# A seventh-product scheme in a down projection: two more groups, and the sums of activations formed earlier

## The chip, the core and the metric

The kernel runs on one core of one Trainium2 chip. The number that counts is the device time of one execution in microseconds (us), the median over repeated runs, lower being better. A core has a matrix engine (PE, with its weight loads shown as PEld), a vector engine (DVE), a scalar engine (ACT), GpSimd (POOL) and SyncE (SP). They run beside each other and wait for one another through semaphores. In this kernel SP issues nearly all loads from HBM, in the order of its own queue, and POOL issues the stores of sums.

## What is computed

One layer of a hybrid transformer block for 256 positions of width 2048: an input projection, three kinds of attention, a gated merge, an output projection, then a feed-forward part. The change lies in the feed-forward part, in its last product and in what prepares it:

```python
h2 = rms_norm(x, g_ffn[l])
u = causal_depthwise_conv(h2 @ w_up[l], conv_w[l], conv_b[l])      # 2048 -> 2 x 5632
u_gate, u_val = jnp.split(u, 2, axis=-1)
x = x + (jax.nn.silu(u_gate) * u_val) @ w_down[l]                  # 5632 -> 2048
```

All of it is in float32. The kernel splits each float32 number into a high and a low float32r part and makes each product of three matmuls: high x high, low x high, high x low.

## The kernel before

**The up projection (L1219, L1221).** The loop runs over 11 blocks of four feature tiles (`f0`), twice each (`s` = 0 for the gate half, 1 for the value half), and over 8 pairs of k tiles: 176 passes, called ticks here. A tick loads 512 KB of weights (`raw_u`, issued by SP at L172, four buffers), ACT casts them to the high part (`hi_u`, L175), DVE subtracts to get the low part (`lo_u`, L176), both in rings of four buffers, and PE runs 16 matmuls. The order of the loads `raw_u` against other loads on SP is left to a scheduler.

**The convolution (`conv`, L1136 to L1163).** After each half of a block two generators are queued, one for each pair of feature tiles; they advance at most one step a tick. ACT and DVE apply taps and bias (`cr`, `u`, `z`, `y`). In the value half DVE multiplies by the gate (L1156) and the result is split into `aT`, which stays in SBUF (L1160, L1163).

**Sums of weights (`weight_sums`, L1177 to L1193).** The down projection treats some pairs of k tiles ("groups") by a scheme with seven products in the place of eight. It needs four sums of weight blocks. Two of them (T4 and T2), or all four, are made on DVE during the up projection: every seventh tick a new group loads its four 128x512 blocks on SP's queue into `r` (first the tile `r[1]` with two buffers, then `r[0]` with one), DVE adds, and POOL stores 512 KB to HBM as `T`. A group with all four (in the set `ALL_FOUR`) has one more add and a store of `r[0]` itself (L1191), so that the next group's loads into `r[0]` have to wait on SP's queue until this store has landed.

**The down projection (L1252 to L1471).** It runs in two halves of 1024 output columns. `PLANS` sets the order by hand: `e` is a group of eight products (`eight`: two loads of 512 KB, 24 matmuls of 128x512), `s` one of seven (`seven`: 21 matmuls, four steps p0 to p3 that prepare weights and u0 to u3 that use them). Steps are prepared two ahead (`AHEAD`). A group without its T1 and T3 in HBM makes them by two adds on DVE (L1371, L1372). The scheme also needs four sums of activations for each pair, its forms. They are made in this stage by `forms(p)`, on DVE and ACT: five adds and subtractions, two casts, two subtractions for the low part (L1273 to L1285). They serve both halves.

Of the kernel before, what the change touches and what calls it, by code (L numbers as in the profile page):

```python
# [37 lines left out]
PLANS = ("eeeee" + "se" * 5 + "sse" + "s" + "eee", "e" + "sse" * 4 + "ssse" + "sssee")  # L38
ALL_FOUR = {(0, 6), (0, 7)} | {(1, p) for p in range(14) if p not in (4, 6, 8, 11)}
# [10 lines left out]
NSEVEN = tuple(plan.count("s") for plan in PLANS)  # L50
# [3 lines left out]
def hybrid_block(  # L54
# [1075 lines left out]
    def conv(ps, f, s):  # L1130
# [20 lines left out]
        if s == 0:  # L1151
            nc.scalar.activation(y, y, AF.Silu)
            ys[f] = y
        else:
            g = ys.pop(f)
            nc.vector.tensor_tensor(g, g, y, ALU.mult)  # L1156
# [6 lines left out]
            nc.vector.tensor_tensor(a[:, :, S:], g, a[:, :, :S].bitcast(F32), ALU.subtract)  # L1163
            ended.append(f)

    ended = []
    made = {}
    asked = [(0, p) for p in range(NSEVEN[0])] + [(1, p) for p in range(NSEVEN[1])]

    def weight_sums(nb, p):  # L1170
# [11 lines left out]
        four = (nb, p) in ALL_FOUR  # L1182
# [24 lines left out]
    for f0 in range(0, FT, 4):  # L1207
        for s in range(2):
            pairs = [two_banks(f"u{f0 + i}_{s}") for i in (0, 2)]
            c0 = s * D_FF + f0 * P  # L1210
            for k in range(0, KT, 2):
# [11 lines left out]
                if asked and n_ticks[0] > 8 and n_ticks[0] % 7 == 2:  # L1223
                    adding.append([weight_sums(*asked.pop(0)), 0])
# [22 lines left out]
    FS3, FS1, FS2, FS4 = range(4)  # L1247
# [8 lines left out]
    def form_of(p, f):  # L1256
        if f == FS4:
            return pieces_of(p)[:, 0, :, 1]
        if p < 10:
            return sf[:, p, f]  # L1260
        return pieces_at(31 - p).rearrange("p k (f l q) -> p (k f) l q", f=2, l=2)[:, f]

    def forms(p):

        flat = aT[:, 2 * p : 2 * p + 3].rearrange("p k s -> p (k s)").bitcast(F32)
        v = flat[:, :1024].rearrange("p (k l t q) -> p k l t q", k=2, l=2, t=NT)
        d = sm.tile([P, 512], F32, tag="junk", bufs=2, name=f"fd_{p}").rearrange("p (f l q) -> p f l q", f=2, l=2)
        r = down_pool().tile([P, 512], F32, tag="fr", bufs=1, name=f"fr_{p}").rearrange("p (f q) -> p f q", f=4)
        g = rbc.rearrange("p (k q) -> p k q", k=2)
        two = flat[:, : 2 * 640].rearrange("p (a b) -> p a b", b=640)[:, :, :512]  # L1270
        two = two.rearrange("p a (l t q) -> p a l t q", l=2, t=NT)[:, :, :, 0]
        tt = nc.vector.tensor_tensor
        keep(tt(d, two, v[:, 0, :, 1].unsqueeze(1).to_broadcast([P, 2, 2, P]), ALU.subtract))  # L1273
        keep(tt(g, v[:, :, 0, 0], v[:, :, 1, 0], ALU.add))
        keep(tt(r[:, :2], d[:, :, 0], d[:, :, 1], ALU.add))
        keep(nc.vector.scalar_tensor_tensor(r[:, FS2], r[:, FS1], -1.0, g[:, 0], ALU.mult, ALU.subtract))
        keep(tt(r[:, FS4], r[:, FS2], g[:, 1], ALU.add))
        yield
        to = sf[:, p] if p < 10 else form_of(p, slice(0, 3))
        last = form_of(p, FS4)  # L1280
        keep(nc.scalar.copy(to[:, :, 0], r[:, :3]))
        keep(nc.scalar.copy(last[:, 0], r[:, FS4]))
        yield
        keep(tt(to[:, :, 1], r[:, :3], to[:, :, 0].bitcast(F32), ALU.subtract))
        keep(tt(last[:, 1], r[:, FS4], last[:, 0].bitcast(F32), ALU.subtract))  # L1285
# [64 lines left out]
    def seven(p, n0, X, Y, first, last):  # L1350
# [3 lines left out]
        four = (n0 // PIECE, p) in ALL_FOUR  # L1354
# [10 lines left out]
        def p2():  # L1365
            raw[2] = load(made[n0 // PIECE, p][0], f"t{name}")
            raw[3] = down_pool().tile([P, PIECE], F32, tag="t13", bufs=2, name=f"t13_{name}")
            if four:
                keep(nc.sync.dma_start(raw[3], made[n0 // PIECE, p][1]))
            else:  # L1370
                keep(nc.vector.tensor_tensor(raw[3][:, :512], raw[0][:, :512], raw[0][:, 512:], ALU.add))  # L1371
                keep(nc.vector.tensor_tensor(raw[3][:, 512:], raw[0][:, 512:], raw[1][:, 512:], ALU.add))  # L1372
            w["T4"], w["T2"] = parts(raw[2], f"t42_{name}")
# [7 lines left out]
        def u1():  # L1381
            three(X()[0][0], *a_of(k1, 0), w["10"])
# [64 lines left out]
    formed = 0  # L1447
# [5 lines left out]
    for nb, plan in enumerate(PLANS):  # L1453
        n0 = nb * PIECE
        ns, s = plan.count("s"), 0
# [3 lines left out]
        if nb == 0:  # L1459
            at(-1, lambda: start(0))  # L1460
        for i, c in enumerate(plan):
            if c == "s":
                seven(s, n0, X, Y, s == 0, s == ns - 1)
                s += 1
                if s == ns:
                    at(len(steps) - 1, lambda nb=nb: later(gather(nb, banks[nb][1])))
            else:
# [4 lines left out]
                if formed < ns and n_done >= 4 - 3 * nb:  # L1472
                    at(len(steps) - 2, lambda p=formed: later(forms(p)))
                    formed += 1
        assert s == ns and not straight and formed >= ns
# [49 lines left out]
```

## Time and profile before

| | |
|---|---|
| device time, median of 3 runs | 1472.15 us (1470.21 to 1473.51) |
| span of the profiled execution (first to last instruction) | 1469.9 us |
| mean granted clock of the matrix engine | 0.999 of full speed |
| busy share of the span: PE, PEld, DVE, ACT, POOL | 100%, 84%, 82%, 61%, 5% |
| up projection's ticks, first matmul to last | about 748 to 1241 us of the span |
| down projection's matmuls | 1241 to 1466 us of the span |
| groups by seven | 8 in the first half, 14 in the second |

The profile gives the span of the profiled execution alone; the runs' times also hold what lies around the span, about 2 us. The page's busy time of PE overlaps neighbouring matmuls, so it says that PE had always something in hand, not that it ran at its peak; the distance between starts is what a matmul costs.

### The profile page before, as it was taken

How to read it: one execution, taken by the hardware profiler on the slowest of the kernel's cores; microseconds unless marked ns; L12 is line 12 of the kernel's file. 1: busy time of each engine (PE TensorE's matmuls, PEld its weight loads, DVE VectorE, ACT ScalarE, POOL GpSimd, SP SyncE). 2: the span in 40 equal slices, each digit the busy share in tenths (PEclk: the TensorE clock that was granted, in tenths of full speed). 3: DMA queues.
4: the chain of work that ended last, by engine and by line, in shares of the span. 5: the costliest groups of instructions: out<-in, count | busy, mean ns of one | idle time of the engine just before them, and what ended most of it. 6: DMA issues, size and time to landing. Idle time of an engine off the chain costs nothing.

```text
span 1469.9 us, 20741 instructions
## 1 busy us (share of the span) xinstructions
PE 1462.8 (100%) x7327; PEld 1233.4 (84%) x7327; DVE 1205.1 (82%) x1617; ACT 895.3 (61%) x1287; POOL 68.8 (5%) x139
## 2 busy tenths in 40 slices
PE   9999999999999999999999999999999999999998
PEld 7888888888878888888888888888888888888887
DVE  5798767766997799888877888788887886998998
ACT  6755454454664466545657667567676777665774
POOL 1000001021000000000000000000000010000000
PEclk9999999999999999999999999999999999999999
DMA  8697898787766576866776888889888895778995
GB/s 295 202 341 260 265 313 270 226 294 267 256 221 204 204 271 247 287 222 237 273 239 218 302 272 276 294 277 310 295 265 273 280 305 190 249 256 286 334 315 191
DMA packets 163463, 388.81 MB, mean 265 GB/s; under 512 B 14016, under 2 KB 22512, under 8 KB 163360
## 3 DMA queue, kind: packets, MB, share of 16 engines
q1 hardware_dynamic: 150960, 345.34, 70.6%
q0 software_dynamic: 11648, 41.10, 7.3%
q8 instruction: 57, 0.93, 0.3%
q10 hardware_dynamic: 752, 1.06, 0.2%
q14 instruction: 46, 0.38, 0.1%
HBM read 349.70 MB, written 37.75 MB: 264 GB/s over the span
## 4 chain that ended last, share of the span: by engine, by line
PE 94%; DVE 3%; DMA 2%; issue 1%; ACT 0%; SPq 0%; DVEq 0%; ACTq 0%
PE u L1219 21%; PE u L1221 10%; PE d L1310 5%; PE d L1309 5%; PE d L1311 5%; PE g_x L769 4%; PE g_x L770 4%; PE g_x L771 4%; PE s L186 2%; PE s L188 2%; PE f L187 2%; PE f L188 2%; PE f L186 2%; PE s L187 2%; PE b L186 2%; PE b L188 2%
## 5 line engine op out<-in xcount | busy, mean ns | idle before, releaser
L1219 PE MATMUL u<-hT,hi_u 128*128 128x512 f32 x1408 | 442.6, 396 | 0.0
L1221 PEld LDWEIGHTS u<-hT,lo_u 128*128 128x128 f32 x1408 | 264.4, 188 | 63.5 <-DVE lo_u L176 1.1
L1221 PE MATMUL u<-hT,lo_u 128*128 128x256 f32 x1408 | 277.0, 278 | 0.7 <-DVE lo_u L176 0.7
L176 DVE TENSOR_TENSOR lo_u<-raw_u,hi_u 128x1024 fp32r<-128x1024 f32 x176 | 213.2, 1220 | 59.8 <-ACT hi_u L175 59.0
L175 ACT CAST hi_u<-raw_u 128x1024 fp32r<-128x1024 f32 x176 | 183.0, 1049 | 107.0 <-PE u L1219 54.6
L1219 PEld LDWEIGHTS u<-hT,hi_u 128*128 128x128 f32 x1408 | 214.5, 189 | 0.1
L764 ACT CAST hi_g<-raw_g 128x1024 fp32r<-128x1024 f32 (+1 forms) x96 | 91.1, 964 | 53.5 <-PE g_x L770 33.4
L765 DVE TENSOR_TENSOR lo_g<-raw_g,hi_g 128x1024 fp32r<-128x1024 f32 (+1 forms) x96 | 105.0, 1116 | 20.9 <-ACT hi_g L764 20.8
L769 PE MATMUL g_x<-hi_g,xT 128*128 128x512 f32 x251 | 98.8, 394 | 0.0
L770 PE MATMUL g_x<-hi_g,xT 128*128 128x512 f32 x251 | 97.7, 389 | 0.0
L771 PE MATMUL g_x<-lo_g,xT 128*128 128x512 f32 x251 | 96.3, 390 | 0.0
L1148 DVE TENSOR_TENSOR y<-y,z 128x512 f32<-128x512 f32 x88 | 60.7, 691 | 24.4 <-ACT z L1147 20.5
L1147 ACT ACTIVATE z<-u,taps 128x256 f32<-128x256 f32 x176 | 74.7, 496 | 0.0
L1309 PE MATMUL d<-hi_d,aT 128*128 128x512 f32 x176 | 68.5, 389 | 0.0
L1310 PE MATMUL d<-hi_d,aT 128*128 128x512 f32 x176 | 68.5, 389 | 0.0
L1311 PE MATMUL d<-lo_d,aT 128*128 128x512 f32 x176 | 68.1, 389 | 0.0
L175 ACT CAST hi_f<-raw_f 128x1024 fp32r<-128x1024 f32 (+1 forms) x40 | 38.6, 968 | 46.6 <-PE f L187 41.9
L186 PE MATMUL s<-hi_s,xT 128*128 128x512 f32 (+1 forms) x160 | 61.9, 387 | 0.0
L175 ACT CAST hi_b<-raw_b 128x1024 fp32r<-128x1024 f32 x32 | 33.6, 1052 | 45.2 <-PE b L187 23.5
L175 ACT CAST hi_s<-raw_s 128x1024 fp32r<-128x1024 f32 (+1 forms) x40 | 38.3, 959 | 36.8 <-PE s L187 29.3
L186 PE MATMUL f<-hi_f,xT 128*128 128x512 f32 (+1 forms) x160 | 60.4, 377 | 0.0
L188 PE MATMUL s<-lo_s,xT 128*128 128x512 f32 (+1 forms) x160 | 59.1, 369 | 0.0
(498 smaller groups left out, 3265.0 us busy)
## 6 DMA issues: line engine op xcount, KB each, us to landing
raw_u<-in_w_up_dram SPq DMA_DIRECT2D x176, 512.0 KB, 5.4
raw_g<-in_w_in_dram SPq DMA_DIRECT2D x86, 512.0 KB, 5.4
T<-r POOLq DMA_DIRECT2D x64, 512.0 KB, 6.1
r<-in_w_down_dram SPq DMA_DIRECT2D x88, 256.0 KB, 5.2
raw_d<-in_w_down_dram SPq DMA_DIRECT2D x44, 512.0 KB, 5.4
raw_f<-in_w_in_dram SPq DMA_DIRECT2D x32, 512.0 KB, 5.5
raw_s<-in_w_in_dram SPq DMA_DIRECT2D x32, 512.0 KB, 5.4
raw_s<-in_w_down_dram SPq DMA_DIRECT2D x32, 512.0 KB, 5.3
```

Source lines behind the costliest of these rows:

```text
L175: pin(nc.scalar.copy(hi[:, :m], raw[:, :m]))
L176: pin(nc.vector.tensor_tensor(lo[:, :m], raw[:, :m], hi[:, :m].bitcast(F32), ALU.subtract))
L186: nc.tensor.matmul(o, lhsT=xh, rhs=wh, start=first, stop=False)
L188: nc.tensor.matmul(o, lhsT=xh, rhs=wl, start=False, stop=last)
L769: nc.tensor.matmul(o, lhsT=a[0], rhs=w[0], start=first, stop=False)
L770: nc.tensor.matmul(o, lhsT=a[1], rhs=w[0], start=False, stop=False)
L771: nc.tensor.matmul(o, lhsT=a[0], rhs=w[1], start=False, stop=last)
L1219: nc.tensor.matmul(ps, lhsT=hi[:, j, c], rhs=hT[:, k + j, :], start=first, stop=False)
L1221: nc.tensor.matmul(ps[:, :S], lhsT=lo[:, j, c], rhs=hT[:, k + j, :S], start=False, stop=last)
L1309: nc.tensor.matmul(o, lhsT=ah, rhs=w[0], start=first, stop=False)
L1310: nc.tensor.matmul(o, lhsT=al, rhs=w[0], start=False, stop=False)
L1311: nc.tensor.matmul(o, lhsT=ah, rhs=w[1], start=False, stop=last)
```

## The change

Five things are done together.

1. The first half gets ten groups by seven (it had eight), the second keeps fourteen; two groups by eight go. The letter in the plan now tells the kind: `t` has two weight sums from HBM and makes the other two, `f` has all four from HBM. There are 15 of `t` and 9 of `f` (before: 10 and 12), all ten of the first half being `t`.
2. A new group of `weight_sums` starts every sixth tick, where it was every seventh.
3. The forms of the first 14 pairs are made in `conv`, from the product before its split, by three instructions on DVE (`unsplit_forms`), written over `y`, and stored by POOL to HBM, 256 KB a pair.
4. In the down projection `forms(i)` loads two pairs' forms with one load of 512 KB on SP's queue and splits them: two casts on ACT, two subtractions on DVE for the two pairs.
5. The two sums of a `t` group are written over its own weights (`raw[0]`) and have no tile of their own; extra load buffers go from two to four and are taken every second time.

```diff
-PLANS = ("eeeee" + "se" * 5 + "sse" + "s" + "eee", "e" + "sse" * 4 + "ssse" + "sssee")
-ALL_FOUR = {(0, 6), (0, 7)} | {(1, p) for p in range(14) if p not in (4, 6, 8, 11)}
+PLANS = ("eeee" + "tte" * 4 + "te" * 2 + "ee", "e" + "ftfe" * 4 + "ft" + "eee")
...
             ended.append(f)
+            if f // 2 < NFORM:
+                yield 1
+                unsplit_forms(f // 2, g, y)
+
+    def unsplit_forms(p, g, y):
+        v = g.rearrange("p k (t q) -> p (k t) q", t=NT)
+        r = y.rearrange("p k (t q) -> p (k t) q", t=NT)
+        tt = nc.vector.tensor_tensor
+        tt(r[:, :2], v[:, 0:4:3], v[:, 1:2].to_broadcast([P, 2, P]), ALU.subtract)
+        nc.vector.scalar_tensor_tensor(r[:, FS2], r[:, FS1], -1.0, v[:, 0], ALU.mult, ALU.subtract)
+        tt(r[:, FS4], r[:, FS2], v[:, 2], ALU.add)
+        if p % 2 == 0:
+            rforms[p // 2] = dram.tile([P, 2, 512], F32, name=f"rform{p}")
+        nc.gpsimd.dma_start(rforms[p // 2][:, p % 2], y.rearrange("p k s -> p (k s)"))
...
-                if asked and n_ticks[0] > 8 and n_ticks[0] % 7 == 2:
+                if asked and n_ticks[0] > 8 and n_ticks[0] % 6 == 2:
...
-        if turn[0] > 10 and turn[0] % 3 == 0:
-            return down_pool().tile([P, PIECE], F32, tag="more", bufs=2, name=name)
+        if turn[0] > 10 and turn[0] % 2 == 0:
+            return down_pool().tile([P, PIECE], F32, tag="more", bufs=4, name=name)
...
+    def forms(i):
+        p = 2 * i
+        n = min(2, NFORM - p)
+        raw = load(rforms[i][:, :n].rearrange("p a n -> p (a n)"), f"fr_{i}")
+        ...
+        yield 2
+        keep(nc.scalar.copy(to[:, :, :, 0], r[:, :, :3]))
+        keep(nc.scalar.copy(last[:, :, 0], r[:, :, FS4]))
+        yield
+        keep(nc.vector.tensor_tensor(to[:, :, :, 1], r[:, :, :3], to[:, :, :, 0].bitcast(F32), ALU.subtract))
+        keep(nc.vector.tensor_tensor(last[:, :, 1], r[:, :, FS4], last[:, :, 0].bitcast(F32), ALU.subtract))
...
         def p2():
-            raw[2] = load(made[n0 // PIECE, p][0], f"t{name}")
-            raw[3] = down_pool().tile([P, PIECE], F32, tag="t13", bufs=2, name=f"t13_{name}")
             if four:
-                keep(nc.sync.dma_start(raw[3], made[n0 // PIECE, p][1]))
+                raw[3] = load(made[n0 // PIECE, p][1], f"t13_{name}")
             else:
-                keep(nc.vector.tensor_tensor(raw[3][:, :512], raw[0][:, :512], raw[0][:, 512:], ALU.add))
-                keep(nc.vector.tensor_tensor(raw[3][:, 512:], raw[0][:, 512:], raw[1][:, 512:], ALU.add))
+                add(raw[0][:, :512], raw[0][:, :512], raw[0][:, 512:])
+                add(raw[0][:, 512:], raw[0][:, 512:], raw[1][:, 512:])
+                raw[3] = raw[0]
+            raw[2] = load(made[n0 // PIECE, p][0], f"t42_{name}")
```

In the built program all engines' instructions stand in the same order as before up to the up projection. Some places show what moves; a name is a tile's with its number, the last digits count tiles.

SP's queue in the up projection, before: the loads of the weight sums' group (1, 5) among the loads of the up projection's weights. The two loads of `r[1]` (`r1`) come first, then the two of `r[0]` (`r0`); the last row is the next group's first.

```order
L1177 DMA r1_1_5_9704<-in_w_down_dram 128x512
L172 DMA raw_u24_0_8_9706<-in_w_up_dram 128x2x512
L1177 DMA r1_1_5_9704<-in_w_down_dram 128x512
L172 DMA raw_u24_0_10_9729<-in_w_up_dram 128x2x512
L172 DMA raw_u24_0_12_9752<-in_w_up_dram 128x2x512
L1177 DMA r0_1_5_9703<-in_w_down_dram 128x512 x2
L172 DMA raw_u24_0_14_9775<-in_w_up_dram 128x2x512
L172 DMA raw_u24_1_0_9799<-in_w_up_dram 128x2x512
L172 DMA raw_u24_1_2_9855<-in_w_up_dram 128x2x512
L172 DMA raw_u24_1_4_9882<-in_w_up_dram 128x2x512
L1177 DMA r1_1_6_9906<-in_w_down_dram 128x512
```

The same queue now, around the same group, which stands elsewhere in the up projection.

```order
L1195 DMA r1_1_5_9858<-in_w_down_dram 128x512
L173 DMA raw_u24_1_0_9862<-in_w_up_dram 128x2x512
L1195 DMA r1_1_5_9858<-in_w_down_dram 128x512
L173 DMA raw_u24_1_2_9918<-in_w_up_dram 128x2x512
L173 DMA raw_u24_1_4_9941<-in_w_up_dram 128x2x512
L173 DMA raw_u24_1_6_9964<-in_w_up_dram 128x2x512
L1195 DMA r0_1_5_9857<-in_w_down_dram 128x512 x2
L173 DMA raw_u24_1_8_9986<-in_w_up_dram 128x2x512
L173 DMA raw_u24_1_10_10010<-in_w_up_dram 128x2x512
L1195 DMA r1_1_6_10038<-in_w_down_dram 128x512
```

Between a group's loads of `r[0]` and the next group's first load now stand two `raw_u`, where there were four.

DVE in the up projection now, at the end of the first block's value half: L1177 to L1179 are the three new instructions for the forms, and they stand between the convolution's own and the `lo_u` that PE waits for.

```order
L1157 TENSOR_TENSOR y_0_0_7114<-y_0_0_7114,y_0_1_7330 128x512
L1138 TENSOR_TENSOR cr_2_1_7344<-cr_2_1_7344,u2_1_7087 128x512
L1177 TENSOR_TENSOR y_0_1_7330<-y_0_0_7114 128x256
L1164 TENSOR_TENSOR aT_6836<-y_0_0_7114,aT_6836 128x2x256
L1139 TENSOR_TENSOR u1_7083<-cr_2_1_7344,rbc_884 128x2x256
L1178 SCALAR_TENSOR_TENSOR y_0_1_7330<-y_0_1_7330,y_0_0_7114 128x128
L177 TENSOR_TENSOR lo_u4_0_10_7470<-raw_u4_0_10_7468,hi_u4_0_10_7469 128x1024
L1179 TENSOR_TENSOR y_0_1_7330<-y_0_1_7330,y_0_0_7114 128x128
```

Before, the rows L1177 to L1179 were not there; now the three come twice in each block of four feature tiles up to the seventh.

DVE in the down projection before, in a seven-product group of the first half, which an eight-product group follows: the forms of a later pair (L1273 to L1277, then L1284 and L1285) and the two sums (L1371, L1372) stand between the low parts of its weights (`lo_s`, `lo_t`).

```order
L1305 TENSOR_TENSOR lo_s0_8_12410<-raw_s0_8_12407,hi_s0_8_12409 128x512
L1273 TENSOR_TENSOR fd_5_12425<-aT_6836 128x512
L1274 TENSOR_TENSOR rbc_884<-aT_6836 128x256
L1275 TENSOR_TENSOR fr_5_12426<-fd_5_12425 128x256
L1276 SCALAR_TENSOR_TENSOR fr_5_12426<-fr_5_12426,rbc_884 128x128
L1277 TENSOR_TENSOR fr_5_12426<-fr_5_12426,rbc_884 128x128
L1305 TENSOR_TENSOR lo_s0_9_12435<-raw_s0_9_12432,hi_s0_9_12434 128x1024
L1371 TENSOR_TENSOR t13_0_4_12454<-raw_s0_8_12407 128x512
L1372 TENSOR_TENSOR t13_0_4_12454<-raw_s0_8_12407,raw_s0_9_12432 128x512
L1305 TENSOR_TENSOR lo_t42_0_4_12458<-raw_t0_4_12452,hi_t42_0_4_12457 128x1024
L1284 TENSOR_TENSOR sf_11814<-fr_5_12426,sf_11814 128x3x128
L1285 TENSOR_TENSOR aT_6836<-fr_5_12426,aT_6836 128x128
```

Seven instructions for one pair's forms stand in one group.

DVE in the down projection now, in the first `t` group of the first half: the subtractions for two loaded pairs of forms (L1303, L1304) and the two sums (L1362) stand between the low parts (`lo_`) of its steps. A second `t` group follows at once.

```order
L1312 TENSOR_TENSOR lo_s0_0_12062<-raw_s0_0_12059,hi_s0_0_12061 128x512
L1312 TENSOR_TENSOR lo_s0_1_12089<-raw_s0_1_12086,hi_s0_1_12088 128x1024
L1303 TENSOR_TENSOR sf_11890<-raw_fr_1_12015,sf_11890 128x6x128
L1304 TENSOR_TENSOR aT_6836<-raw_fr_1_12015,aT_6836 128x2x128
L1362 TENSOR_TENSOR raw_s0_0_12059<-raw_s0_0_12059 128x512
L1362 TENSOR_TENSOR raw_s0_0_12059<-raw_s0_0_12059,raw_s0_1_12086 128x512
L1312 TENSOR_TENSOR lo_t42_0_0_12119<-raw_t42_0_0_12116,hi_t42_0_0_12118 128x1024
L1312 TENSOR_TENSOR lo_t13_0_0_12126<-raw_s0_0_12059,hi_t13_0_0_12125 128x1024
```

For two pairs there are two instructions, and the sums are written over the loaded weights.

More of the change, by code (lines that the diff above doesn't have):

```diff
@@ L49 @@
 OUT_SEVENS = 3
-NSEVEN = tuple(plan.count("s") for plan in PLANS)
+KINDS = tuple(plan.replace("e", "") for plan in PLANS)
+NSEVEN = tuple(len(kinds) for kinds in KINDS)
+NFORM = max(NSEVEN)
 @with_exitstack
@@ L1164, in conv @@
             ended.append(f)
+            if f // 2 < NFORM:
+                yield 1
+                unsplit_forms(f // 2, g, y)
+    FS3, FS1, FS2, FS4 = range(4)
+    rforms = {}
+    def unsplit_forms(p, g, y):
[8 more added lines that the diff above has]
+        nc.gpsimd.dma_start(rforms[p // 2][:, p % 2], y.rearrange("p k s -> p (k s)"))
     ended = []
     made = {}
-    asked = [(0, p) for p in range(NSEVEN[0])] + [(1, p) for p in range(NSEVEN[1])]
+    asked = [(nb, p) for nb in range(2) for p in range(NSEVEN[nb])]
     def weight_sums(nb, p):
@@ L1181, in weight_sums @@
         add = lambda o, i: tc.keep_in_program_order(nc.vector.tensor_tensor(o, o, i, ALU.add))
-        four = (nb, p) in ALL_FOUR
+        four = KINDS[nb][p] == "f"
         add(r[0][:, 0], r[0][:, 1])
@@ L1258, in form_of @@
             return pieces_of(p)[:, 0, :, 1]
[L1259 to L1285, printed above, removed]
+        return sf[:, p % 10, f]
     turn = [0]
@@ L1298, in load @@
         return raw
+    def forms(i):
+        p = 2 * i
+        n = min(2, NFORM - p)
+        raw = load(rforms[i][:, :n].rearrange("p a n -> p (a n)"), f"fr_{i}")
+        r = raw.rearrange("p (a f q) -> p a f q", a=2, f=4)[:, :n]
+        to = sf[:, p % 10 : p % 10 + n]
+        last = aT[:, 2 * p : 2 * (p + n)].rearrange("p (a k) (l t q) -> p a k l t q", k=2, l=2, t=NT)[:, :, 0, :, 1]
+        yield 2
[4 more added lines that the diff above has]
+        keep(nc.vector.tensor_tensor(last[:, :, 1], r[:, :, FS4], last[:, :, 0].bitcast(F32), ALU.subtract))
+        issued.update((f"forms{p}", f"forms{p + 1}"))
     def parts(src, name):
@@ L1353, in seven @@
         w, raw = {}, {}
-        four = (n0 // PIECE, p) in ALL_FOUR
+        four = KINDS[n0 // PIECE][p] == "f"
+        add = lambda o, a, b: keep(nc.vector.tensor_tensor(o, a, b, ALU.add))
         def p0():
@@ L1381, in u1 @@
         def u1():
+            assert f"forms{p}" in issued
             three(X()[0][0], *a_of(k1, 0), w["10"])
@@ L1454, in hybrid_block @@
         n0 = nb * PIECE
-        ns, s = plan.count("s"), 0
+        ns, s = NSEVEN[nb], 0
         X, Y = (lambda nb=nb: banks[nb][0]), (lambda nb=nb: banks[nb][1])
@@ L1460, in hybrid_block @@
             at(-1, lambda: start(0))
+            for i in range(5):
+                at((0, 3, 6, 13, 23)[i], lambda i=i: later(forms(i)))
         for i, c in enumerate(plan):
-            if c == "s":
+            if c != "e":
                 seven(s, n0, X, Y, s == 0, s == ns - 1)
+                if nb and s % 2 and s // 2 + 5 < (NFORM + 1) // 2:
+                    at(len(steps), lambda i=s // 2 + 5: later(forms(i)))
                 s += 1
@@ L1471, in hybrid_block @@
                     at(len(steps) - 1, lambda nb=nb: residual(nb))
[L1472 to L1475, printed above, removed]
+        assert s == ns and not straight
         at(len(steps) - 1, finish)
```

2 lines of the change are left out of this document (removed).

## The prediction

> **What bounds the kernel now.** I read the page first (busy shares, the chain that ended last), then the busy time by stretches, then the waits inside the up and the down projection.
>
> ```profile
> span 1469.9 us, 20741 instructions
> PE 1462.8 (100%) x7327; PEld 1233.4 (84%) x7327; DVE 1205.1 (82%) x1617; ACT 895.3 (61%) x1287; POOL 68.8 (5%) x139
> PE 94%; DVE 3%; DMA 2%; issue 1%; ACT 0%; SPq 0%; DVEq 0%; ACTq 0%
> ```
>
> PE has something in hand for all but 7 us, and the chain is matmuls for 94%. So time is saved only by matmuls left out, and lost only where PE comes to wait. The stretches (columns: length, busy PE, PEld, DVE, ACT, POOL, granted clock, DMA share, GB/s): the first is from the up projection, the rest from the down projection.
>
> ```profile
> 1002.00:1174.00 172.00, 172.00 (x990) 150.06 (x989) 141.32 (x171) 120.42 (x189) 6.92 (x13) 1.00 0.85 283
> 1241.00:1353.00 112.00, 112.00 (x496) 92.79 (x496) 104.38 (x148) 70.29 (x92) 0.00 (x0) 1.00 0.74 254
> 1353.00:1465.70 112.70, 112.64 (x497) 92.95 (x496) 104.23 (x139) 70.72 (x83) 4.33 (x8) 1.00 0.81 285
> 1281.00:1301.00 20.00, 20.00 (x90) 16.58 (x89) 19.80 (x30) 12.49 (x17) 0.00 (x0) 1.00 0.75 257
> 1361.00:1381.00 20.00, 20.00 (x90) 16.57 (x89) 18.70 (x25) 14.69 (x18) 1.95 (x4) 1.00 0.99 374
> ```
>
> PE never idles in the down projection, though DVE is busy 93% of it and 99% of one stretch. A tick of the up projection is 172 / 990 x 16 = 2.78 us, with DVE busy for 141.32 / 172 = 82% (2.28 us a tick). The up projection has one visible gap, after the matmuls that start at 986.51; PE's timeline shows it, and the chain says what led there.
>
> ```profile
> 986.51 0.63 PE L1219 MATMUL u<-hT,hi_u 128*128 128x512 f32 x2
> 987.82 0.50 PE L1221 MATMUL u<-hT,lo_u 128*128 128x256 f32 x2 [0.68 <-DVE lo_u L176]
> ```
>
> ```profile
> 969.72 7.04 DMA raw_u<-in_w_up_dram
> 976.86 1.06 ACT hi_u L175
> 986.63 1.15 DVE lo_u L176
> ```
>
> Two 512-wide matmuls take 0.46 us from start to start elsewhere, here 1.31, so PE lost about 0.84 us. A load came late (7.04 us), and DVE, busy with the convolution and weight sums, delivered `lo_u` just too late. The lead that the four buffers allow was used up once.
>
> **The change, part by part.** *Matmuls.* The down projection has 22 x 21 + 22 x 24 = 990 matmuls in 224.7 us, 0.227 us each. Two groups turned from eight to seven products leave out 2 x 3 = 6: -1.36 us. PE's instructions before that stage are the same.
>
> *DVE in the up projection.* Rows of this stretch, mean ns after the total:
>
> ```profile
> L176 DVE TENSOR_TENSOR lo_u<-raw_u,hi_u 128x1024 fp32r<-128x1024 f32 x176 | 213.2, 1220 | 59.8 <-ACT hi_u L175 59.0 <-PE u L1221 0.2
> L175 ACT CAST hi_u<-raw_u 128x1024 fp32r<-128x1024 f32 x176 | 183.0, 1049 | 107.0 <-PE u L1219 54.6 <-DMA raw_u<-in_w_up_dram 37.9 <-PE o_x L770 7.0
> L1148 DVE TENSOR_TENSOR y<-y,z 128x512 f32<-128x512 f32 x84 | 58.0, 691 | 23.1 <-ACT z L1147 19.2
> L1138 DVE TENSOR_TENSOR u<-cr,rbc 128x512 f32<-128x512 f32 x42 | 28.9, 689 | 0.9
> L1137 DVE TENSOR_TENSOR cr<-cr,u 128x512 f32<-128x512 f32 x42 | 28.6, 682 | 5.9 <-ACT cr L1136 5.9
> L1156 DVE TENSOR_TENSOR y<-y,y 128x512 f32<-128x512 f32 x20 | 13.7, 686 | 0.1
> L1163 DVE TENSOR_TENSOR aT<-y,aT 128x512 fp32r<-128x512 f32 x20 | 13.7, 684 | 0.0
> L1181 DVE TENSOR_TENSOR r<-r 128x512 f32<-128x512 f32 x44 | 30.2, 686 | 0.4
> ```
>
> Forms and sums share DVE with these. The down projection's old forms give the new ones' prices:
>
> ```profile
> L1273 DVE TENSOR_TENSOR fd<-aT 128x512 f32<-128x512 f32 x14 | 9.6, 684 | 0.0
> L1274 DVE TENSOR_TENSOR rbc<-aT 128x256 f32<-128x256 f32 x14 | 5.9, 418 | 0.0
> L1276 DVE SCALAR_TENSOR_TENSOR fr<-fr,rbc 128x128 f32<-128x128 f32 x14 | 4.1, 292 | 0.5
> L1284 DVE TENSOR_TENSOR sf<-fr,sf 128x384 fp32r<-128x384 f32 x10 | 5.5, 550 | 0.0
> L1285 DVE TENSOR_TENSOR aT<-fr,aT 128x128 fp32r<-128x128 f32 x14 | 4.0, 283 | 0.0
> ```
>
> One pair's forms are a subtraction of 128x256 (0.42) and two instructions of 128x128 (0.29 each): 1.00 us, 14 us in all. The groups' adds go from 78 to 24 x 3 + 9 = 81: 2.1 us more, but closer together. All of it lies beside matmuls as long as the lead lasts. In the eight ticks of a value half (22.3 us) DVE now does 8 x 1.22 + two convolutions of 4.12 (six instructions of 0.68 to 0.69) + 8/7 x 3.7 adds x 0.69 = 20.9 us. After it does 2.0 more for forms and 8/6 x 3.64 x 0.69 = 3.3 for sums: 23.3 us, 1.0 more than it has. The gate half that follows has 3.7 us to spare (9.76 + 5.5 + 3.3 of 22.3). So DVE isn't the bound on the whole, but the lead dips by some 2.4 us more in seven value halves (blocks with forms). One dip reached zero before. I take three of the seven to run short by the 0.84 us seen: 2.5 us. The bounds are 0 (the lead holds) and 7 x 2.4 = 17 us (it is at zero each time). The low value is nearer to the rows, since one gap in 22 halves is all that shows. The 0.84 us gap itself is left out: its place is newly mixed.
>
> *Order on SP's queue.* The next rows are waits in the up projection (us in total, times, longest).
>
> ```profile
> SPq L1177 <- DMA T<-r: 48.9, 17, 5.7
> ACT hi_u L175 <- PE u L1219: 54.6, 41, 2.6
> ACT hi_u L175 <- DMA raw_u<-in_w_up_dram: 37.9, 24, 4.6
> ```
>
> SP stood 48.9 us in front of loads into `r`, waiting for a store of sums; all `raw_u` behind had to stand too. Casts found no free buffer 41 times (PE well supplied), and 24 times waited for a load. One group with four sums, from DVE's adds through POOL's store to the next group's loads and the first `raw_u` behind them:
>
> ```profile
> 1035.80 0.69 DVE L1181 TENSOR_TENSOR r<-r 128x512 f32<-128x512 f32 x1
> 1037.51 0.53 POOL L1191 DMA_DIRECT2D T<-r  x1 [16.26 <-DVE r L1181]
> 1043.19 1.03 SPq L1177 DMA_DIRECT2D r<-in_w_down_dram  x2
> 1044.32 5.27 SPq L172 DMA_DIRECT2D raw_u<-in_w_up_dram  x4
> 1051.45 1.23 DVE L176 TENSOR_TENSOR lo_u<-raw_u,hi_u 128x1024 fp32r<-128x1024 f32 x1 [0.25 <-ACT hi_u L175]
> ```
>
> From the first add (1035.80) to the end of that `lo_u` (1052.68) it is 16.9 us. In the new order the next `f` group's first add stands right behind this `lo_u`. The loop has to fit into six ticks, 16.7 us, where it had seven, 19.5. It just doesn't: 0.2 us for each of the nine `f` groups, of which four are followed by another `f`. I set 0 in the sum, for the lead and the `t` groups between can take this; the price is open upward, and this is the main rival below.
>
> The median store of sums, by the page's issue row:
>
> ```profile
> T<-r POOLq DMA_DIRECT2D x64, 512.0 KB, 6.1
> ```
>
> The loop's store took 5.7 us. The Trainium skill ("DMA: Bandwidth & Descriptors", section "Anatomy of one DMA") fits a GpSimd DMA by about 2.0 us plus bytes over 436 GB/s. By this a 512 KB store takes an estimated 3.2 us; the loop would be 14.4 us, and six ticks would hold it with 2.3 us to spare. The trace does not agree with it here: its stores share the DMA engines with the loads.
>
> *Traffic.* Six ticks move 3.15 MB of `raw_u`, 1.05 of `r`, on average 0.86 of `T` and 0.2 of forms: 5.26 MB in 16.7 us, 315 GB/s, where 283 took a share of 0.85. In proportion 0.95. The down projection once moved 374 GB/s at 0.99 with PE at full pace. So it fits; landings get later, not earlier. No term.
>
> *The down projection.* DVE loses the old forms (the five rows above alone are 29 us) and gets seven pairs of subtractions, 1.37 us each (768 columns between 384 at 0.55 and 1024 at 1.22, and 0.42). PE didn't wait for it, so this gains nothing. What is new is two `t` groups in a row with loaded forms between:
>
> ```profile
> L1305 DVE TENSOR_TENSOR lo_s<-raw_s,hi_s 128x512 fp32r<-128x512 f32 (+1 forms) x44 | 41.8, 953 | 2.5 <-ACT hi_s L1304 2.2 <-issue 0.3
> L1305 DVE TENSOR_TENSOR lo_t<-raw_t,hi_t 128x1024 fp32r<-128x1024 f32 x22 | 26.9, 1222 | 2.0 <-ACT hi_t L1304 1.1
> L1371 DVE TENSOR_TENSOR t<-raw_s 128x512 f32<-128x512 f32 x10 | 6.8, 684 | 0.0
> ```
>
> A `t` costs DVE 2 x 0.95 + 2 x 1.22 + 2 x 0.68 = 5.7 us, `tte` 2 x 5.7 + 2 x 1.22 = 13.9, beside 66 x 0.227 = 15.0 of PE. The first `tte` has two loads of forms in it (16.6: 1.6 over), the second one (15.3: 0.3 over). Between 0 (the stretch at 99% without a gap) and 1.9 I take 0.7. ACT's new casts, POOL's 14 stores and SP's seven loads cost nothing: ACT has 35% free, POOL 95%, and the forms are stored at least 100 us before they are loaded. If that cover is gone, a load of forms that waits for a buffer would hold the weights behind it.
>
> **Sum.** 1469.9 - 1.36 - 0.84 + 2.5 + 0.7 = 1470.9 us of span. Around the span lie 2.2 us (the median 1472.15 less 1469.9): 1473.15, say **1473.2 us**, 0.07% above the median. A measurement of this kernel can tell about 0.2%, 2.9 us, from no change.
>
> **Rivals.** *All covered (0.26).* Leads hold everywhere: 1472.15 - 1.36 = 1470.8, or 1469.95 if the old gap goes too. For it: PE never idled at 99% DVE, and 41 casts waited for PE alone; the skill's shorter store would give this too. Against it: the gap at 987 and SP's 48.9 us.
>
> *The store-to-load loop binds (0.34): slower.* Place: `r[0]`'s next load on SP's queue. With the higher DMA share the landings of store and `raw_u` lengthen. By one us together, the loop is 17.9, 1.2 us over in each of nine `f` groups: 10.8, less a lead that can be used once (four buffers give at most three ticks less a cast and a `lo_u`, 8.3 - 2.3 = 6 us; dips leave about 4 of it): 7 us, 1472.15 - 2.2 + 7 = 1477. From 0.6 us over in each group (a loop of 17.3, the median store) it decides: nine times 0.6 less 2.2 is +3. Against it: `t` groups between let the lead recover.
>
> *Faster beyond 0.2% (0.04).* It would need 2.9 us; the matmuls and the gap give 2.2.
>
> **Chances.** The forecast (leads run out in places, 1471 to 1475) 0.36, all covered 0.26, the loop 0.34, faster 0.04. Within 0.2% are the first two: 0.62; slower 0.34; faster 0.04. The range goes from all covered, 1469.8, to the loop's case with 2 us on top, 1479; about 0.1 is left out above and below each.
>
> **What would show it.** In the profile after: 984 matmuls in the down projection at 0.227 us; DVE near 88% and a DMA share near 0.94 in the middle of the up projection; PE gaps of 0.5 to 1.5 us in value halves, ended by `lo_u`; SP's wait for `T` at 40 to 80 us. Wrong it would be if SP's waits for stores pass 100 us with gaps in each run of `f` groups, or if PE has no gap at all.

## The result and the profile after

| | before | changed |
|---|---|---|
| median device time | 1471.47 us (1470.21 to 1473.51, 4 runs) | 1483.67 us (1480.80 to 1484.78, 4 runs) |
| ratio, 95% interval | | 1.0076 [1.0061, 1.0091] |
| span of the profiled execution | 1469.9 us | 1479.1 us |
| up projection, from its first matmul to the down projection's first | 493.45 us | 495.58 us |
| down projection, from its first matmul to the end of its last | 224.59 us (990 matmuls) | 230.91 us (984) |

The change made the kernel slower by 0.76% (the ratio is the estimate over all runs; the two medians alone give 1.0083). The profiled execution is the shortest of the four; the others had spans of 1481.6 to 1483.1 us at mean granted clocks of 0.997 to 0.998, where it had 0.999.

Its span is 9.2 us longer: 6.3 in the down projection, 2.1 in the up projection, 1.1 ahead of both (a load comes late there in some executions, also of the old code; the up projection starts between 747.0 and 749.7 us in the executions kept), less 0.4 in the tail. The page's first lines and its chain that ended last:

```profile
span 1479.1 us, 20788 instructions
PE 1465.8 (99%) x7321; PEld 1231.6 (83%) x7321; DVE 1201.2 (81%) x1592; ACT 895.0 (61%) x1277; POOL 76.0 (5%) x152
PE 78%; DMA 7%; DVE 7%; issue 4%; ACT 3%; SPq 0%; POOL 0%; DVEq 0%; ACTq 0%; POOLq 0%
```

The busy shares hardly moved. The chain did: PE's part fell from 94% to 78%, so PE came to wait, but neither line says where. The busy time by stretches does (columns as in the prediction):

```profile
1002.00:1174.00 172.00, 171.23 (x979) 148.10 (x978) 148.75 (x192) 120.47 (x188) 11.26 (x21) 1.00 0.91 308
1241.00:1353.00 112.00, 107.67 (x466) 86.99 (x465) 92.10 (x103) 70.34 (x88) 2.16 (x4) 0.98 0.82 281
1353.00:1475.20 122.20, 122.17 (x540) 100.82 (x538) 102.14 (x114) 70.83 (x78) 4.32 (x8) 1.00 0.79 283
1266.00:1270.00 4.00, 1.62 (x6) 0.68 (x5) 1.06 (x1) 2.17 (x3) 0.00 (x0) 1.00 0.98 394
1270.00:1275.00 5.00, 3.20 (x12) 2.09 (x12) 4.92 (x7) 2.40 (x5) 0.00 (x0) 1.00 0.52 180
1275.00:1279.00 4.00, 3.94 (x11) 3.04 (x11) 3.66 (x6) 2.31 (x3) 0.00 (x0) 0.57 0.81 270
```

The first half of the down projection lost 4.3 us of PE's time, nearly all of it between 1266 and 1275. Behind it the granted clock fell to 0.57 for a while, so that 11 matmuls filled 4 us in which 17 to 18 fit at 0.227. Four rows of PE's own timeline there (the bracket is the idle time before, and what ended it):

```profile
1266.50 0.39 PE L1318 MATMUL d<-lo_s,aT 128*128 128x512 f32 x1
1268.96 0.50 PE L1316 MATMUL d<-hi_s,aT 128*128 128x512 f32 x1 [2.07 <-ACT hi_s L1311]
1270.22 0.50 PE L1318 MATMUL d<-lo_s,aT 128*128 128x512 f32 x1 [0.53 <-DVE lo_s L1312]
1273.90 0.50 PE L1316 MATMUL d<-hi_t,sf 128*128 128x512 f32 x1 [1.58 <-ACT hi_t L1311]
```

The chain of waits through the same place leads from the first of these gaps back to a load, and from the load to DVE's subtraction of *forms*, at L1304:

```profile
1259.24 0.34 DVE aT L1304
1259.61 8.16 DMA raw_s<-in_w_down_dram
1267.86 1.05 ACT hi_s L1311
1268.94 1.22 DVE lo_s L1312
```

L1304 is the last reader of a loaded buffer of forms. SP's queue (first column: when the load was issued) shows when that buffer had been taken:

```profile
1235.53 0.33 SPq L1288 DMA_DIRECT2D raw_fr<-rform  x1
1238.21 5.90 SPq L1288 DMA_DIRECT2D raw_d<-in_w_down_dram  x3
1248.13 0.33 SPq L1288 DMA_DIRECT2D raw_fr<-rform  x1
1252.31 3.27 SPq L1288 DMA_DIRECT2D raw_d<-in_w_down_dram  x2
1258.40 0.33 SPq L1288 DMA_DIRECT2D raw_s<-in_w_down_dram  x1
1258.82 0.38 SPq L1288 DMA_DIRECT2D raw_fr<-rform  x1
1259.61 0.33 SPq L1288 DMA_DIRECT2D raw_s<-in_w_down_dram  x1
1259.98 0.49 SPq L1288 DMA_DIRECT2D raw_t<-T  x1
1262.52 1.05 SPq L1288 DMA_DIRECT2D raw_s<-in_w_down_dram  x2
1271.44 0.33 SPq L1288 DMA_DIRECT2D raw_t<-T  x1
```

Up to its eleventh turn `buffer()` gives nothing but the ring of four; every even turn after that gives an extra buffer (`more`). The first two loads of forms are turns 4 and 8: the first held one of the four from 1235.5 to 1259.6 (24 us; the `raw_s` at 1259.61 comes at its release), the second one from 1248.1 to 1271.4 (23 us; the `raw_t` at 1271.44 comes at its release). The third, from 1258.8 to 1277.3, is turn 12 and took an extra buffer. So from 1248.1 to 1259.6 the loads of weights had two buffers left, and three until 1271.4. They went out late and then at once: six loads between 1258.4 and 1263.6, which landed at 394 GB/s in the 4 us from 1266. The one that PE waited for took 8.16 us.

In the up projection the leads got thinner. All of it, by waits (total, times, longest), and SP's wait for stores of sums:

```profile
ACT hi_u L176 <- DMA raw_u<-in_w_up_dram: 71.1, 50, 6.8
ACT hi_u L176 <- PE u L1237: 27.6, 22, 2.0
SPq L1195 <- DMA T<-r: 79.6, 24, 6.3
```

Casts waited for a load 50 times (24 before), for PE 22 times (41). PE's longest gap there, 0.91 us of idle time, and the chain ahead of it:

```profile
991.91 0.50 PE L1239 MATMUL u<-hT,lo_u 128*128 128x256 f32 x2 [0.91 <-DVE lo_u L177]
...
986.44 1.14 DVE lo_u L177
987.57 0.60 DVE y L1157
988.17 0.60 DVE r L1199
988.77 0.34 DVE y L1177
989.11 0.60 DVE aT L1164
989.71 0.20 DVE y L1178
...
990.43 0.28 DVE y L1179
990.72 1.15 DVE lo_u L177
```

DVE is busy nearly throughout: adds for sums (L1199) and the three new instructions (L1177 to L1179) stand between one `lo_u` and the next. Five gaps (from start to start 1.31, 0.53, 0.35, 1.03 and 0.40 us where 0.23 is usual) cost 2.5 us together. The last of the three new instructions ends at 1088.7 us, so three of the gaps (1098, 1124 and 1150, 1.1 us together) lie behind all work on forms.

### The profile page after: what moved, and what is told of

It is laid out like the page before. It is cut to its first block, busy times and chain, and to the rows that moved or that the text cites. A ratio compares the mean times of both kernels' runs of the same rounds, so it can differ in the third digit from the quotient of the medians.

```text
span 1479.1 us, 20788 instructions
## 1 busy us (share of the span) xinstructions
PE 1465.8 (99%) x7321; PEld 1231.6 (83%) x7321; DVE 1201.2 (81%) x1592; ACT 895.0 (61%) x1277; POOL 76.0 (5%) x152
## 3 DMA queue, kind: packets, MB, share of 16 engines
q10 hardware_dynamic: 752, 1.06, 0.2%
## 4 chain that ended last, share of the span: by engine, by line
PE 78%; DMA 7%; DVE 7%; issue 4%; ACT 3%; SPq 0%; POOL 0%; DVEq 0%; ACTq 0%; POOLq 0%
PE u L1237 15%; PE u L1239 8%; PE d L1318 4%; PE d L1316 4%; PE d L1317 4%; PE g_x L770 4%; PE g_x L771 4%; PE g_x L772 4%; DMA raw_u<-in_w_up_dram 2%; PE f L188 2%; PE f L187 2%; PE f L189 2%; PE b L187 2%; PE b L189 2%; PE b L188 2%
## 5 line engine op out<-in xcount | busy, mean ns | idle before, releaser
L1316 PE MATMUL d<-hi_d,aT 128*128 128x512 f32 x160 | 62.3, 389 | 0.0
L1317 PE MATMUL d<-hi_d,aT 128*128 128x512 f32 x160 | 62.3, 389 | 0.0
L1318 PE MATMUL d<-lo_d,aT 128*128 128x512 f32 x160 | 61.4, 389 | 0.0
```

What stands on the lines that cost most here:

```text
L1316: nc.tensor.matmul(o, lhsT=ah, rhs=w[0], start=first, stop=False)
L1317: nc.tensor.matmul(o, lhsT=al, rhs=w[0], start=False, stop=False)
L1318: nc.tensor.matmul(o, lhsT=ah, rhs=w[1], start=False, stop=last)
```

## The experiments

Theory A: in the down projection the buffers that the forms occupy hold back the weights. Rivals: DVE's work order in the `t` pairs; for the up projection the store-to-load loop of the prediction, or DVE's fill by forms and by closer sums. Stage lengths below come from one profiled execution of each kernel, ratios from all its runs against the kernel before on the same chip. All four programs here that have the old up projection give 492.5 to 493.5 us for it, so differences under 1 us in a stage say little.

### The loads of forms moved, left out, or kept without their work

Moved, nothing else:

```diff
-                at((0, 3, 6, 13, 23)[i], lambda i=i: later(forms(i)))
+                at((0, 12, 22, 32, 42)[i], lambda i=i: later(forms(i)))
```

> Changed kernel, with the five loads of forms in the first half moved from after steps 0, 3, 6, 13, 23 to after steps 0, 12, 22, 32, 42; all work kept. Theory A (the early loads of forms sit in the ring of four load buffers while the down projection starts, so that the weights come late and in a bunch): the gaps at 1266 to 1281 us go, the down projection takes 223.5 to 225 us (230.9 in the changed kernel), the time falls by 6 to 10 us to about 1474 to 1477. Theory B (the forms' subtractions and the sums of two t groups in a row overload DVE): part of the gap stays at the first pair of t groups, 226 to 229 us, since the second load still falls into it. Theory C (all of the loss is in the up projection): no change.

Measured: ratio 1.0007 [0.9998, 1.0016], median 1473.58 us; down projection 223.57 us, which is 984 x 0.227. The stretch that had the stall:

```profile
1266.00:1285.00 19.00, 18.98 (x84) 15.38 (x83) 18.72 (x21) 12.70 (x15) 0.00 (x0) 1.00 0.95 342
```

PE has no gap left there beyond 0.2 us. Of the 0.76%, 0.69 go with the places of the loads. The first load of forms still stands after step 0 in this kernel and held its buffer of the ring for 22.6 us (1237.27 to 1259.90). One buffer missing cost nothing; in the changed kernel two were missing at once.

Then the first three loads left out, with the same work on other data:

```diff
-        raw = load(rforms[i][:, :n].rearrange("p a n -> p (a n)"), f"fr_{i}")
+        if i < 3:
+            raw = aT[:, 24:26].rearrange("p k s -> p (k s)").bitcast(F32)
+        else:
+            raw = load(rforms[i][:, :n].rearrange("p a n -> p (a n)"), f"fr_{i}")
```

> Changed kernel; the first three loads of forms are left out and their casts and subtractions read other data of the same shape already in SBUF, at the same places. The forms of the first six pairs are so not those of the reference. Theory A: no buffer is held and six loads are not bunched, so the down projection takes 223.5 to 225 us. Theory B: DVE and ACT do all the work of before, so at least half of the 7 us stays (227 us or more).

Measured: 1.0024 [1.0014, 1.0034]; down projection 226.50 us. The stall at 1266 shrank to one gap of 0.5 us; what remains is at the change of halves (1389 to 1401, about 2 us). So it missed theory A's 223.5 to 225 us by 1.5, at a place that this edit doesn't touch, and stayed under theory B's 227.

And the loads kept at their places, but the casts and subtractions of the first three cut to one column:

```diff
+        if i < 3:
+            keep(nc.scalar.copy(to[:, 0, 0, 0, :1], r[:, 0, 0, :1]))
+            yield
+            keep(nc.vector.tensor_tensor(to[:, 0, 0, 1, :1], r[:, 0, 0, :1], to[:, 0, 0, 0, :1].bitcast(F32), ALU.subtract))
```

> Changed kernel; the first three loads of forms are made, but of the casts and subtractions on them one column is left (the forms of the first six pairs are zeros set by GpSimd in place of the reference's). Theory A: the buffers are still held as long, by the one column that stands in the same place, so at least 4 of the 7 us stay in the down projection (228 us or more). Theory B: the overload is gone, 223.5 to 225 us.

Measured: 1.0053 [1.0036, 1.0071]; down projection 231.91 us, with the stall in its old place (1.0, 2.4 and 0.9 us from start to start between 1266 and 1272) and matmuls at half speed behind it. The work without the loads hardly has a stall there, the loads without the work have it. DVE's order in the `t` pairs is not the cause.

### Sums every seventh tick

```diff
-                if asked and n_ticks[0] > 8 and n_ticks[0] % 6 == 2:
+                if asked and n_ticks[0] > 8 and n_ticks[0] % 7 == 2:
```

> Changed kernel with a new group of weight sums at every seventh tick again (24 groups, the last at tick 170). If six ticks are what made PE wait in the up projection, that stage falls from 495.6 us to about 493.5 and its gaps of 0.3 to 1.1 us near 990, 1008 and 1123 us go; if the forms' three instructions did it, it stays at 495 to 496. The down projection stays at 229 to 233 us under theory A, whose cause lies in its own first steps.

Measured: 1.0069 [1.0053, 1.0084]; SP's wait for stores fell from 79.6 to 36.5 us, the up projection to 494.60 us, the down projection stayed at 233.64, with 2.9 us from start to start at 1265. Of the gaps named beforehand none is left, but two stand at 810 and 814 us instead (1.7 us together). The closer spacing isn't what made the kernel slower.

### The up projection's 2 us

With the loads of forms moved as in the first experiment, three variants: sums every seventh tick; sums every sixth tick, but the three DVE instructions of `unsplit_forms` left out (its stores stay); sums every seventh tick with no `f` group.

```diff
-        tt(r[:, :2], v[:, 0:4:3], v[:, 1:2].to_broadcast([P, 2, P]), ALU.subtract)
-        nc.vector.scalar_tensor_tensor(r[:, FS2], r[:, FS1], -1.0, v[:, 0], ALU.mult, ALU.subtract)
-        tt(r[:, FS4], r[:, FS2], v[:, 2], ALU.add)
```

```diff
-PLANS = ("eeee" + "tte" * 4 + "te" * 2 + "ee", "e" + "ftfe" * 4 + "ft" + "eee")
+PLANS = ("eeee" + "tte" * 4 + "te" * 2 + "ee", "e" + "tte" * 3 + "ttte" * 2 + "tt" + "ee")
```

> Loads of forms late (as in the run with them after steps 0, 12, 22, 32, 42) and a new group of weight sums at every seventh tick. If the six-tick spacing costs the up projection one to two of its 2 to 3 us, that stage takes 494 to 495 us and the time falls 1 to 2 us below the late loads alone (1473.6), to 1472 to 1473, level with the kernel before. If the spacing costs nothing and the forms' instructions do it, the up projection stays near 496 us and the time near 1473.6.

> Loads of forms late, six ticks; the three DVE instructions that make the forms in the convolution are left out (the stores to HBM stay, of other numbers, so the forms are not those of the reference). If these instructions make PE run short in the value halves, the up projection falls from 495.6 to 496.9 us to 494 us or less; if SP's waits for stores do it, it stays at 495 us or more.

> Loads of forms late, seven ticks, and the second half's 14 seven-product groups all of the kind with two sums from HBM (in the order e, three times tte, twice ttte, tt, ee). No store of r[0] is left, so if SP's wait for it is what makes loads late, that wait falls from 36 us to under 15 us and the up projection takes 493.5 to 494.2 us. The second half has more adds on DVE (5.7 us a group beside 4.8 of PE): if DVE is the rival bound there, the down projection grows from 223.6 us by 1 to 3 us.

Measured, with SP's wait for stores and how often casts waited for PE (many: PE well supplied):

| kernel | up projection | down projection | SP's wait | casts on PE | ratio |
|---|---|---|---|---|---|
| changed | 495.58 us | 230.91 us | 79.6 us | 22 | 1.0076 |
| loads moved | 496.86 | 223.57 | 88.1 | 27 | 1.0007 [0.9998, 1.0016] |
| moved, and seventh tick | 493.58 | 226.97 | 31.5 | 47 | 0.9995 [0.9986, 1.0004] |
| moved, and no DVE forms | 492.96 | 224.15 | 81.8 | 37 | 0.9998 [0.9988, 1.0008] |
| moved, and seventh tick, no `f` | 494.92 | 225.57 | 10.9 | 54 | 1.0020 [1.0011, 1.0029] |

Without the forms' DVE work there is no loss, though SP waits for stores as long as ever; with next to no wait for stores there still are gaps (so the last row missed its 493.5 to 494.2 us; its down projection is 2.0 us longer than with the loads moved alone, within the 1 to 3 us given for DVE's added sums). The chain ahead of this last kernel's longest gap (1.06 us of idle time at 988.70) is DVE's work, and no store:

```profile
985.63 0.68 DVE y L1149
986.31 0.07 DVE r L1199
986.38 0.45 issue
986.83 0.68 DVE y L1157
987.51 1.15 DVE lo_u L177
```

In the changed kernel, too, no store stands in the chains ahead of the three longest gaps. But it isn't so everywhere. With the loads moved (496.86 us, the longest of all) the chain ahead of a gap of 0.98 us at 1196.18 does go through a store of sums and the `raw_u` that SP held back behind it:

```profile
1175.21 6.45 DMA T<-r
...
1182.88 6.66 DMA raw_u<-in_w_up_dram
...
1194.99 1.14 DVE lo_u L177
```

The same holds for the gap of 1.05 us at 1078.97 there. So the store-to-load loop is not needed for a gap, but it takes part in some. Taking the profiled executions of all these kernels together: sixth tick with forms 494.4 to 496.9 us (five kernels), seventh tick with forms 493.6 to 494.9 (four), sixth tick without forms 493.0 (one), before 492.5 to 493.5 (four). Forms and closer spacing together cost some 2 to 3 us by the profiles, of which the spacing is about half; with executions scattering by 1 us this split is rough. By the ratios it is less: without the forms' instructions 0.09% are gained, 1.3 us, with intervals that overlap. How much of the spacing's part goes through DVE and how much through the stores was not separated, nor how the forms' instructions bear on gaps behind the last of them.

### Held buffers in the kernel before

This adds to the kernel *before* three loads of 512 KB at the places of the new ones, each held until DVE copies one column of it (by their turns the first two take buffers of the ring, the third an extra one, as in the changed kernel). Nothing else of the change is in it.

```diff
+    def hold(i):
+        raw = load(made[0, i][0], f"hold_{i}")
+        yield 2
+        yield
+        keep(nc.vector.tensor_copy(sm.tile([P, 16], F32, tag="nwa", name=f"held_{i}")[:, :1], raw[:, :1]))
+
+    for i in range(3):
+        at((0, 3, 6)[i], lambda i=i: later(hold(i)))
```

> The kernel before, with three loads of 512 KB added after steps 0, 3 and 6 of the down projection into its ring of load buffers, each held until one column is copied by DVE three to four steps later. Nothing else changes, the forms are made as before. Theory A (held buffers alone make the weights late): the down projection grows from 224.6 us by 2 to 8 us, with PE gaps around the first group by seven. Theory B (DVE's new order) expects no gap, 224.6 to 225.

Measured: 1.0043 [1.0028, 1.0058]; down projection 231.25 us, 6.7 more than before, with gaps at 1270 to 1276 and at 1284 to 1289.

Two things are still together in that, the traffic and the occupied buffer. First the traffic alone, with copies from HBM to HBM that take no buffer:

```diff
+    def copy(i):
+        keep(nc.sync.dma_start(dram.tile([P, PIECE], F32, name=f"copied_{i}"), made[0, i][0]))
+        yield
```

> This is the kernel before with three copies of 512 KB from HBM to HBM, issued by SP after the steps 0, 3 and 6 of the down projection, the places at which the changed kernel loads its first forms (the output does not depend on them). They bring at least the traffic of those loads and stand as long on SP's queue, but occupy no buffer of the load ring. Theory A (the occupied buffer holds back the weights): no stall at 1266 to 1285, the down projection within 1 us of the kernel before (224.6 us), ratio 1.000 (0.999 to 1.001). Rival D (the traffic of three more loads, bunched with the weights, is what comes too late): a stall of 3 to 7 us in the down projection, ratio 1.002 to 1.005.

Then the held loads again, but released at once by GpSimd:

```diff
-        yield 2
-        yield
-        keep(nc.vector.tensor_copy(sm.tile([P, 16], F32, tag="nwa", name=f"held_{i}")[:, :1], raw[:, :1]))
+        keep(nc.gpsimd.tensor_copy(sm.tile([P, 16], F32, tag="nwa", name=f"held_{i}")[:, :1], raw[:, :1]))
+        yield
```

> The kernel before with the same three loads of 512 KB into the load ring as in the run that held them, after steps 0, 3 and 6, but each buffer is given back at once: GpSimd, which has nothing else to do there, copies one column as soon as the load has landed. Traffic and places on SP's queue are those of the held run (down projection 231.3 us, ratio 1.0043); a buffer is occupied for some 5 to 6 us instead of 11 to 25. Theory A, in the form that the time for which a buffer is held counts: the down projection 224.6 to 227 us, ratio 0.999 to 1.0015. Rival: a buffer taken at all, however short, costs a load of weights its turn: 229 to 232 us, ratio 1.003 to 1.005.

Measured: 1.0001 [0.9991, 1.0010] with the down projection at 224.59 us for the copies, 0.9997 [0.9987, 1.0007] and 224.57 us for the short loads. No gap appears in either. The two loads of the held kernel that took buffers of the ring, issue and release:

```profile
1233.17 0.33 SPq L1297 DMA_DIRECT2D raw_hold<-T  x1
...
1245.77 0.33 SPq L1297 DMA_DIRECT2D raw_hold<-T  x1
...
1256.38 0.14 DVE L1484 COPY held<-raw_hold 128x1 f32<-128x1 f32 x1
...
1266.52 0.14 DVE L1484 COPY held<-raw_hold 128x1 f32<-128x1 f32 x1
```

The same of the kernel that releases at once:

```profile
1232.77 0.33 SPq L1297 DMA_DIRECT2D raw_hold<-T  x1
...
1241.02 0.33 SPq L1297 DMA_DIRECT2D raw_hold<-T  x1
...
1237.14 1.11 POOL L1482 COPY held<-raw_hold 128x1 f32<-128x1 f32 x1 [41.26 <-DMA raw_hold<-T]
1246.90 0.18 POOL L1482 COPY held<-raw_hold 128x1 f32<-128x1 f32 x1 [8.65 <-DMA raw_hold<-T]
```

The buffers were held for 23 and 21 us in the one, for 5.5 and 6.1 in the other (with the copy), with the same three loads. So neither the traffic nor the place on SP's queue costs anything; the time for which the buffers are held does. In the held kernel the two times overlap for 11 us, as in the changed kernel, and with the early release they don't. Together with the one buffer held for 22.6 us at no cost in the first experiment this points to two buffers of four being gone at once; whether one held alone would cost something elsewhere was not tried.

### The second half's loads moved too

The seventh-tick version above still lost 3 us in the down projection around the change of halves, where two more loads of forms stand. There a load was issued at 1390.81, right behind the `lo_s` that freed its buffer, and then took 7.60 us. With the loads moved alone the same two loads stand at the same places and the profile has no gap there (223.57 us), so such gaps come in some executions only (2 us of them also with three loads left out); the seventh-tick version's profile is that of its slowest run (1474.06 us, median 1471.09). These two loads were moved to later groups, once with the seventh tick and once with the sixth:

```diff
-                if nb and s % 2 and s // 2 + 5 < (NFORM + 1) // 2:
-                    at(len(steps), lambda i=s // 2 + 5: later(forms(i)))
+                if nb and s in (5, 7):
+                    at(len(steps), lambda i=s // 2 + 3: later(forms(i)))
```

> Loads of forms late in the first half (steps 0, 12, 22, 32, 42), seven ticks, and in the second half the two loads of forms after the sixth and eighth seven-product group in place of the second and fourth, away from the stores and loads of residuals at the change of halves. If loads bunched there make the 3 us of gaps between 1374 and 1400 us seen with the loads late in the first half alone, the down projection takes 223.5 to 224.5 us (227.0 there) and the time falls by 1 to 2 us, to 0.1 to 0.2% below the kernel before. If the gaps come from the residuals' traffic alone, they stay and the time stays level with the kernel before.

> The same with a new group of weight sums at every sixth tick. Six against seven ticks on one chip: if the sums' closer spacing and the forms together overfill DVE in the value halves, the up projection is 1 to 2 us longer than with seven (495 to 496.5 against 493.6 to 494.6) and so is the time; if the spacing is free, both agree within 0.5 us.

Measured: 1.0009 [1.0000, 1.0018] and 1.0013 [1.0004, 1.0022]. The gaps at 1374 to 1400 went, and the down projection took 225.00 and 225.09 us instead of 226.97 (223.5 to 224.5 were expected), with smaller gaps now at 1408 and 1423. The up projection took 493.83 us with the seventh tick and 495.05 with the sixth, as expected for a spacing that costs 1 to 2 us, but the ratios differ by 0.04% alone, inside their intervals. The profiled spans, 1471.4 and 1471.1 us, are 1 us shorter than that of the seventh-tick version (1472.4, its slowest execution), but the ratios, taken on another chip, are 0.14 and 0.18% higher, where a gain of 0.1 to 0.2% was expected. What does this was not found; that the gaps at the change of halves come in some executions only may be why nothing was gained, but not why time was lost. It is at the edge of what these runs resolve. No version was faster than the kernel before beyond its interval.

## Why the prediction was wrong

It said 1473.2 us, at most 1479; measured were 1483.67. The main rival, the store-to-load loop, foretold a slower kernel too, but by way of the up projection, and the larger part was lost in the down projection.

**The step that failed is the sentence that SP's seven loads cost nothing, with the term of +0.7 for the down projection.** With the matmuls left out the prediction has 0.7 - 1.4 = -0.7 us for this stage; the profiled execution has +6.3. These 7 us are most of the 8.2 us by which the profiled span misses the 1470.9 of the sum. The loads were priced as issues and as traffic, and both do cost nothing (1.0001 with the copies). The third thing that a load uses was not priced: a buffer, from its issue until its last reader is done, and for the first two loads that was one of the ring's four. The sentence behind it, that a load of forms waiting for a buffer would hold the weights, named the queue and the buffers, but turned round: the first two loads of forms kept two of the four buffers for 24 and 23 us, since their subtractions stand late in DVE's order, and the weights waited for a buffer. The rows for it were there: the ring of four in the code, the loads' places after the steps 0, 3 and 6, and the turn at which extra buffers begin.

**The clock.** Some 1.9 us of the 7 are slow matmuls (seven at 0.43 us from start to start, two at 0.46 and 0.49). Nothing in the prediction stood for this. In the other executions of the changed kernel the mean clock was lower still by 0.001 to 0.002. Of 1480 us that is an estimated 1.5 to 3 us, part of the 2.5 to 4.0 by which their spans are longer; where the rest lies is open, since they left no trace.

**DVE in the `t` pairs: 0, not 0.7.** With the loads moved all of that work fits (223.57 us). The price of the work itself was right: 0.95 and 0.42 us for two pairs.

**The matmuls: right.** 984 of them, at 0.227 us but for the nine slow ones.

**DVE in the up projection: the size was right, in part by luck, the place only in part.** The term was +2.5, three gaps of 0.84 us in blocks with forms; five gaps of 0.12 to 1.08 us were lost, 2.5 in all, and the two for which the profile names an end were ended by `lo_u`. With the old gap taken off the prediction had +1.7 net, the profile +2.1. But the 0.84 us came from a gap that the other three programs with the old up projection don't have, and three of the five gaps lie behind all work on forms. The halves were mixed up, too: the convolution of a value half is worked off in the ticks of the gate half that follows. The new instructions first run at 802.9 us, in such a half, and the two longest gaps lie in gate halves. The new instructions cost 0.42 + 0.29 + 0.29 us, as taken from the old forms. DVE was busy for 86% of the middle stretch (88% was foretold), the DMA share was 0.91 (0.94).

**The loop: the right wait, the wrong consequence.** SP's wait for stores came out at 79.6 us, at the upper end of the 40 to 80 given for the forecast. But a wait of SP is paid from the lead of four buffers, and with 81.8 us of it and no forms on DVE the stage ran as before. It shows ahead of two gaps with the loads moved, 2.4 us together, and ahead of none of the three longest in the changed kernel.

## What to carry to other kernels

A load added to a shared ring has three prices: its place on the queue, its bytes, and the time from its issue to its last reader's end, during which the ring is one buffer shorter. The third is read from the order of the engine that reads it last: here two loads that held two of four buffers for 21 to 24 us, 11 of them together, cost 7 us; held for 5.5 and 6.1 us they cost nothing, nor did one held alone for 22.6 us. So a load that goes ahead of need into a ring should be placed by its reader, or be given a buffer of its own, which wasn't tried here for the first two.

## What the runs showed of the hardware

The matrix engine's clock fell to half after idle pieces of 2.07, 0.53 and 1.58 us with some matmuls between them (1266.9 to 1273.9), and stayed there for about 3.4 us. The Trainium skill, TensorE: Matmul & The Clock Gate, section "Why this matters for your kernels", advises against idle gaps of over about 3 us. The trace does not agree that gaps have to be so long: the longest here was 2.07 us. What counts shows in the traces' lists of clock changes. In all fourteen traces kept, the clock changes only at whole multiples of 3.413 us from the list's first entry; in the changed kernel it does so after 372, 373 and 432 of them. These are the two steps around the first change (columns as before):

```profile
1271.90:1275.31 3.41, 1.77 (x7) 0.82 (x6) 3.12 (x4) 2.50 (x4) 0.00 (x0) 1.00 0.80 280
1275.31:1278.72 3.41, 3.41 (x9) 2.65 (x10) 3.27 (x5) 2.00 (x3) 0.00 (x0) 0.50 0.77 250
```

PE was busy for 1.77 of 3.41 us, and the next step has half the clock. Two other kernels have such a step in the down projection, those with the loads without their work and with sums every seventh tick; there PE was busy for 0.95 and 0.92 us of the step ahead. In the kernel before with held buffers PE was busy for only 2.51 of the 5 us from 1270, but they fall on two steps, of which the emptier one has 2.06, and the clock stayed up:

```profile
1271.56:1274.97 3.41, 2.06 (x8) 1.41 (x9) 3.41 (x7) 2.33 (x3) 0.00 (x0) 1.00 0.13 31
```

So PE's busy share of one such step goes before a change, and not the longest gap. Where the line lies these rows don't tell: the changed kernel's step from 1265.07 with 1.82 us busy was not followed by half the clock, nor was one with 1.62 us at the end of the seventh-tick version with the loads moved (from 1466.80).

Three more loads need not bring more bytes. Between 1228 and 1266 us the three loads raised the rate from 218 to 284 GB/s when they gave their buffers back at once (the copies raised it to 257), and only to 223 when they held them. With the buffers held SP issued 13 loads of weights and sums between 1226 and 1266 us, where the kernel before issued 16: the ring, short of buffers, let fewer go ahead.
